# Linear attention on one core: the second matmul 128 wide, the output stored in 1 KB runs

## The chip, the cores and the metric

The kernel runs on one core of a Trainium2 chip. The metric is the device time of one execution in microseconds (us). All runs told here were in the fast state. Every profiled run is one execution; times are medians over several. Ratios of two kernels are computed as the mean time of one kernel's fast runs over the mean of the other's in the same rounds, with a 95% interval, so they are not quite the ratio of the medians quoted beside them. Two words are used throughout: a run is a stretch of contiguous bytes in DRAM, and a packet is one record of a DMA engine in the trace, which may carry several runs (the 5632 runs of the GpSimd stores of before went in 2816 packets).

## The reference

For each of 8 x 12 = 96 heads, with 512 rows of 64 elements in Q, K and V (fp32):

```python
Q_feat = np.maximum(0, Q) + 1
K_feat = np.maximum(0, K) + 1
KV = np.einsum('bhkd,bhkv->bhdv', K_feat, V)
K_sum = np.sum(K_feat, axis=2)
numerator = np.einsum('bhqd,bhdv->bhqv', Q_feat, KV)
denominator = np.einsum('bhqd,bhd->bhq', Q_feat, K_sum)
return (numerator / (denominator[:, :, :, None] + 1e-10)).astype(np.float32)
```

It reads 37.75 MB and writes 12.58 MB.

## The kernel before

Twelve groups of eight heads. Loads go from GpSimd's queue and cast fp32 to bf16 on the way: 16 rows of a head per partition, so runs of 4 KB in DRAM. Q is transposed on TensorE; ScalarE copies the transposes from PSUM to `qt`, and the second matmul takes slices of `qt` as its stationary operand. The order in which `qt` is filled decides how many consecutive rows of a head meet in one output partition: with two row halves interleaved it is eight rows, 2 KB of fp32.

```python
        qt = mid_pool.tile([P, C, P, 2], BF16, name="qt")          # C = 8
        for half in range(2):
            qt_ps = psum_qt.tile([P, C, P], BF16, name="qt_ps")
            for c in range(C):
                nc.tensor.transpose(qt_ps[:, c, :], qf[:, half * C + c, :, :], identity)
            nc.scalar.copy(out=qt[:, :, :, half], in_=qt_ps)        # every second element
# ... (output: 32 matmuls of 64 columns per group, then on VectorE
#      4 reciprocals and 4 multiplies into o_sb [P, 4, 8, 64] fp32) ...
    def store(g):
        o_sb = outs.pop(g)
        o_to = o_dram[:, g * NP : g * NP + NP]      # runs of C rows: 2 KB
        if g < NG - 1:
            nc.gpsimd.dma_start(out=o_to, in_=o_sb) # eleven of these
            return
        for h in range(2):                          # last group: two halves from SP
            nc.sync.dma_start(out=o_to[:, h:NP:2], in_=o_sb[:, h:NP:2])
```

A store of group g is issued three groups after its features were made, and up to eight GpSimd DMAs are in flight (19.4 to 19.9 us from issue to landing, at 2.485 us for each). So of the eleven GpSimd stores about four run between loads (60 to 103 us), and the others, with the two SP stores, follow one another after the last load. That last part I call the pure-store stretch.

Of the kernel before, what the change touches and what calls it, by code (L numbers as in the profile page):

```python
# [8 lines left out]
FP32 = mybir.dt.float32  # L9
BF16 = mybir.dt.bfloat16  # L10
ALU = mybir.AluOpType

BANK = 512
# [5 lines left out]
@with_exitstack  # L19
def kernel(  # L20
    ctx: ExitStack,
    tc: tile.TileContext,
    Q: bass.AP,
    K: bass.AP,
    V: bass.AP,
    out: bass.AP,
):






    nc = tc.nc

    B, H, S, D = Q.shape
    P = 128
    C = 8
    C2 = 2 * C
    NPAIR = B * H * S // (P * C)  # L40
    NP = 4
    NG = NPAIR // NP
    D1 = D + 1
    W = 2 * D1

    def view(t, c):
        return t.flatten_outer_dims().rearrange("(n p c) d -> p n c d", p=P, c=c)

    q_dram = view(Q, C2)
    k_dram = view(K, C2)  # L50
    v_dram = view(V, C2)
    o_dram = view(out, C)

    const = ctx.enter_context(tc.tile_pool(name="const", bufs=1))
    head_pool = ctx.enter_context(tc.tile_pool(name="head_pool", bufs=1))
    in_pool = ctx.enter_context(tc.tile_pool(name="in_pool", bufs=IN_BUFS))
    feat_pool = ctx.enter_context(tc.tile_pool(name="feat", bufs=2))
    mid_pool = ctx.enter_context(tc.tile_pool(name="mid", bufs=3))
    out_pool = ctx.enter_context(tc.tile_pool(name="out_pool", bufs=OUT_BUFS))
    recip_pool = ctx.enter_context(tc.tile_pool(name="recip", bufs=4))  # L60
    psum = ctx.enter_context(tc.tile_pool(name="psum", bufs=3, space=bass.MemoryType.PSUM))
    psum_qt = ctx.enter_context(tc.tile_pool(name="psum_qt", bufs=2, space=bass.MemoryType.PSUM))

    identity = const.tile([P, P], BF16, name="identity")
    NV = 2
    v_aug = [const.tile([P, C2, W], BF16, name=f"v_aug{i}") for i in range(NV)]
    kva_diag = [const.tile([P, 4, 2, D1], BF16, name=f"kva_diag{i}") for i in range(NV)]

    raw = {}
    feat = {}  # L70
    qts = {}
    outs = {}

    def load(g):
        first = g == 0
        k_raw = (head_pool if first else in_pool).tile(
            [P, 2, C2, D], FP32 if first else BF16, name="k_raw"
        )
        v_raw = in_pool.tile([P, 2, C2, D], BF16, name="v_raw")
        q_raw = in_pool.tile([P, 2, C2, D], BF16, name="q_raw")  # L80
        (nc.sync if first else nc.gpsimd).dma_start(  # L81
            out=k_raw, in_=k_dram[:, g * 2 : g * 2 + 2]
        )
        nc.gpsimd.dma_start(out=v_raw, in_=v_dram[:, g * 2 : g * 2 + 2])  # L84
        nc.gpsimd.dma_start(out=q_raw, in_=q_dram[:, g * 2 : g * 2 + 2])  # L85
        raw[g] = (k_raw, v_raw, q_raw)

    def store(g):
        o_sb = outs.pop(g)
        o_to = o_dram[:, g * NP : g * NP + NP]  # L90
        if g < NG - 1:
            nc.gpsimd.dma_start(out=o_to, in_=o_sb)  # L92
            return
        for h in range(2):
            nc.sync.dma_start(out=o_to[:, h:NP:2], in_=o_sb[:, h:NP:2])

    def feature(dst, src):
        nc.vector.tensor_scalar(  # L98
            out=dst, in0=src, scalar1=1.0, scalar2=1.0, op0=ALU.add, op1=ALU.max
        )  # L100

    def features(g):
        k_raw, v_raw, q_raw = raw.pop(g)
        kf = feat_pool.tile([P, C2, 2, D], BF16, name="kf")
        qf = feat_pool.tile([P, C2, 2, D], BF16, name="qf")
        va = v_aug[g % NV]
        for half in range(2):
            cs = slice(half * C, half * C + C)
            feature(kf[:, cs].rearrange("p c n d -> p n c d"), k_raw[:, :, cs])
            nc.scalar.copy(  # L110
                out=va[:, cs].rearrange("p c (n x) -> p n c x", n=2)[:, :, :, 0:D],
                in_=v_raw[:, :, cs],
            )
        for half in range(2):
            cs = slice(half * C, half * C + C)
            feature(qf[:, cs].rearrange("p c n d -> p n c d"), q_raw[:, :, cs])
        feat[g] = (kf, qf)

    def kv_and_transpose(g):
        kf, qf = feat.pop(g)  # L120
        va = v_aug[g % NV]
        kva_ps = [psum.tile([P, 2, BANK], FP32, tag="ps", name="kva_ps") for _ in range(2)]
        for c in range(C2):
            for b in range(4):
                ps = slice(32 * b, 32 * b + 32)
                nc.tensor.matmul(  # L126
                    kva_ps[b // 2][:, b % 2, 0:W],
                    lhsT=kf[ps, c, :, :],
                    rhs=va[ps, c, :],
                    start=(c == 0),  # L130
                    stop=(c == C2 - 1),
                )
        kva = kva_diag[g % NV]
        for n in range(2):
            ps = slice(64 * n, 64 * n + 64)
            for h in range(2):
                nc.scalar.copy(  # L137
                    out=kva[ps, 2 * h : 2 * h + 2, n, :],
                    in_=kva_ps[h][ps, :, D1 * n : D1 * n + D1],
                )  # L140

        qt = mid_pool.tile([P, C, P, 2], BF16, name="qt")
        for half in range(2):
            qt_ps = psum_qt.tile([P, C, P], BF16, name="qt_ps")
            for c in range(C):
                nc.tensor.transpose(qt_ps[:, c, :], qf[:, half * C + c, :, :], identity)  # L146
            nc.scalar.copy(out=qt[:, :, :, half], in_=qt_ps)  # L147
        qts[g] = qt

    def output(g):  # L150
        kva = kva_diag[g % NV]
        qt = qts.pop(g)
        o_sb = out_pool.tile([P, NP, C, D], FP32, name="o_sb")
        for h in range(2):
            ops = [psum.tile([P, 2, BANK], FP32, tag="ps", name="o_ps") for _ in range(2)]
            for c in range(C):
                for j in range(2):
                    b = 2 * h + j
                    nc.tensor.matmul(  # L159
                        ops[c // 4][64 * j : 64 * j + 64, c // 2 % 2, (c % 2) * W : (c % 2) * W + W],  # L160
                        lhsT=qt[:, c, 32 * b : 32 * b + 32, :],
                        rhs=kva[:, b],
                        start=True,
                        stop=True,
                    )
            for i in range(2):
                cells = ops[i][:, :, 0 : 2 * W].rearrange("p b (c n x) -> p b c n x", n=2, x=D1)
                recip = recip_pool.tile([P, 2, 2, 2, 1], FP32, name="recip")
                nc.vector.reciprocal(out=recip, in_=cells[:, :, :, :, D:D1])  # L169
                nc.vector.tensor_tensor(  # L170
                    out=o_sb[:, h:NP:2, 4 * i : 4 * i + 4].rearrange(
                        "p n (b c) d -> p b c n d", b=2
                    ),
                    in0=cells[:, :, :, :, 0:D],
                    in1=recip.to_broadcast([P, 2, 2, 2, D]),
                    op=ALU.mult,
                )
        outs[g] = o_sb

    with tc.manual_schedule():  # L180
        for g in range(IN_BUFS):
            load(g)
            if g == 0:
                make_identity(nc, identity)
                for t in kva_diag:
                    nc.gpsimd.memset(t, 0.0)  # L186
                for t in v_aug:
                    nc.gpsimd.memset(t[:, :, D::D1], 1.0)  # L188
        for g in range(NG - 1):
            features(g)  # L190
            if g >= 1:
                kv_and_transpose(g - 1)
            if g >= 2:
                output(g - 2)
            if g + IN_BUFS < NG:
                load(g + IN_BUFS)
            if g >= LAG:
                store(g - LAG)
        kv_and_transpose(NG - 2)
        output(NG - 3)  # L200
        features(NG - 1)
        output(NG - 2)
        kv_and_transpose(NG - 1)
        output(NG - 1)
        for g in range(NG - 1 - LAG, NG):
            store(g)
# [30 lines left out]
```

## Time and profile before

| | before |
|---|---|
| median time | 128.35 us (127.55 to 128.37, 3 runs) |
| span in the profile | 126.5 us |
| share of the span: PE, ACT, DVE | 53%, 51%, 45% |
| GpSimd's DMA queue, share of 16 engines | 99.9% |
| ScalarE copy to qt | 1298 ns |
| last multiply ends / last DMA packet ends | 118.84 / 125.21 us |

Read it from the last row upwards: the compute engines are idle about half of the time, the DMA engines hardly ever, and the end comes 6 us after the last computation. The lines themselves stand in the prediction.

One more view of before will be the yardstick, since most of what follows happens from 108 to 120 us. It is the busy time of the engines in that stretch. Its columns are the stretch, its length, PE, PEld, DVE, ACT and POOL busy (with instruction counts), then the TensorE clock, the DMA share and the GB/s moved:

```profile
108.00:120.00 12.00, 5.93 (x120) 4.67 (x118) 5.53 (x13) 3.31 (x6) 0.75 (x1) 0.64 1.03 415
```

The DMA share of 1.03 says that all 16 engines have packets open throughout; 415 GB/s is what they move with nothing but stores.

### The profile page before, as it was taken

The page shows a single profiled execution, that of the slowest core. Times are in us where ns is not written, and L with a number is a line of the kernel's source. Part 1 is how long each engine was busy: PE and PEld are TensorE (multiplying, and loading weights), DVE is VectorE, ACT ScalarE, POOL GpSimd, SP SyncE. Part 2 cuts the span into 40 slices and gives each one's busy share as a digit, 9 for nine tenths or more (in the row PEclk, how much of TensorE's full clock was granted, in tenths as well). Part 3 has the DMA queues.
Part 4 walks back from the last instruction along what each step waited for, and adds up shares of the span by engine and source line. Part 5 has one row for each costly group of instructions (what it writes and reads, how often), then busy time and mean ns, then how long its engine had stood idle before and what let it go on. Part 6 is the DMA issues. An engine that isn't in the chain of part 4 may idle for free.

```text
span 126.5 us, 3107 instructions
## 1 busy us (share of the span) xinstructions
PE 67.4 (53%) x1344; PEld 54.8 (43%) x1344; DVE 57.3 (45%) x144; ACT 64.1 (51%) x97; POOL 35.2 (28%) x56
## 2 busy tenths in 40 slices
PE   0009139147949486674648547737916972674000
PEld 0009028036838275562537435626714851563000
DVE  0122222058292865919377067147229079805500
ACT  4041095393966939397590492293096592073000
POOL 6992233222332242233223322332221202010000
PEclk9999999999995958679985555555555577569555
DMA  3999999999999999999999999999999999999990
GB/s 75 340 211 208 212 211 213 208 212 210 214 208 211 212 209 214 209 215 208 251 336 212 229 358 209 212 365 214 210 338 249 215 306 418 420 422 405 409 356 33
DMA packets 13341, 32.17 MB, mean 254 GB/s; under 512 B 784, under 2 KB 784, under 8 KB 13328
## 3 DMA queue, kind: packets, MB, share of 16 engines
q0 software_dynamic: 12512, 29.89, 99.9%
q1 hardware_dynamic: 816, 2.10, 4.6%
q8 instruction: 10, 0.16, 0.5%
q14 instruction: 3, 0.02, 0.0%
HBM read 37.75 MB, written 12.58 MB: 398 GB/s over the span
## 4 chain that ended last, share of the span: by engine, by line
DMA 61%; DVE 13%; PE 8%; POOL 5%; issue 3%; ACT 2%; ACTq 1%; POOLq 0%; DVEq 0%
DMA q_raw<-in_Q_dram 46%; DMA v_raw<-in_V_dram 15%; DVE o_sb L170 9%; PE kva_ps L126 5%; PE qt_ps L146 2%; DVE recip L169 2%; DVE qf L98 2%; POOL v_raw L84 1%; POOL q_raw L85 1%; ACT qt L147 1%; POOL k_raw L81 1%; ACTq L232 1%; ACT v_aug L110 1%; PE o_ps L159 1%; POOL kva_diag L186 1%
## 5 line engine op out<-in xcount | busy, mean ns | idle before, releaser
L110 ACT COPY v_aug<-v_raw 128x1024 bf16<-128x1024 bf16 x24 | 24.1, 1056 | 40.5 <-DMA v_raw<-in_V_dram 40.4
L159 PE MATMUL o_ps<-kva_diag,qt 128*64 128x130 bf16 x384 | 22.9, 269 | 26.7 <-ACT kva_diag L137 15.9
L126 PE MATMUL kva_ps<-v_aug,kf 32*128 32x130 bf16 x768 | 24.6, 294 | 22.8 <-ACT v_aug L110 13.0
L170 DVE TENSOR_TENSOR o_sb<-o_ps,recip 128x512 f32<-128x512 f32 x48 | 33.2, 691 | 1.7
L126 PEld LDWEIGHTS <-kf 32*128 32x128 bf16 x768 | 19.7, 132 | 26.9 <-issue 14.6
L159 PEld LDWEIGHTS <-qt 128*64 128x64 bf16 x384 | 16.6, 137 | 32.7 <-issue 19.1
L147 ACT COPY qt<-qt_ps 128x1024 bf16<-128x1024 bf16 x24 | 29.5, 1298 | 0.5
L98 DVE TENSOR_SCALAR qf<-q_raw 128x1024 bf16<-128x1024 bf16 x24 | 9.4, 434 | 39.0 <-DMA q_raw<-in_Q_dram 39.0
L146 PE MATMUL qt_ps<-identity,qf 128*128 128x128 bf16 x192 | 21.4, 301 | 0.0
L146 PEld LDWEIGHTS <-qf 128*128 128x128 bf16 x192 | 18.5, 140 | 2.3 <-issue 2.0
L92 POOL DMA_DIRECT2D out_dram<-o_sb x11 | 8.4, 767 | 27.9 <-DVE o_sb L170 13.6
L98 DVE TENSOR_SCALAR kf<-k_raw 128x1024 bf16<-128x1024 bf16 (+1 forms) x24 | 9.7, 446 | 12.2 <-DMA k_raw<-in_K_dram 12.2
L137 ACT CAST kva_diag<-kva_ps 64x130 bf16<-64x130 f32 x48 | 10.2, 262 | 9.1 <-PE kva_ps L126 8.8
L169 DVE RECIPROCAL recip<-o_ps 128x8 f32<-128x8 f32 x48 | 9.5, 197 | 8.7 <-PE o_ps L159 8.7
L84 POOL DMA_DIRECT2D v_raw<-in_V_dram x12 | 8.7, 726 | 16.8 <-ACT kva_diag L137 7.3
L85 POOL DMA_DIRECT2D q_raw<-in_Q_dram x12 | 8.6, 720 | 15.8 <-DMA q_raw<-in_Q_dram 5.3
L81 POOL DMA_DIRECT2D k_raw<-in_K_dram x11 | 7.9, 714 | 15.4 <-DMA v_raw<-in_V_dram 8.2
L110 ACT ACT_TABLE_LOAD x1 | 1.3, 1283 | 0.7 <-PEq L221 0.7
L186 POOL MEMSET kva_diag<- 128x520 bf16 x2 | 1.0, 528 | 0.0
L188 POOL MEMSET v_aug<- 128x32 bf16 x2 | 0.4, 278 | 0.0
masks.py:199 POOL TENSOR_SCALAR_AFFINE_SELECT identity<-identity 128x128 bf16<-128x128 bf16 x1 | 0.3, 288 | 0.1
masks.py:197 POOL MEMSET identity<- 128x128 bf16 x1 | 0.2, 232 | 0.0
(4 smaller groups left out, 0.4 us busy)
## 6 DMA issues: line engine op xcount, KB each, us to landing
out_dram<-o_sb POOLq DMA_DIRECT2D x11, 1024.0 KB, 19.9
v_raw<-in_V_dram POOLq DMA_DIRECT2D x12, 512.0 KB, 19.4
q_raw<-in_Q_dram POOLq DMA_DIRECT2D x12, 512.0 KB, 19.4
k_raw<-in_K_dram POOLq DMA_DIRECT2D x11, 512.0 KB, 19.4
k_raw<-in_K_dram SPq DMA_DIRECT2D x1, 1024.0 KB, 4.9
out_dram<-o_sb SPq DMA_DIRECT2D x2, 512.0 KB, 6.9
```

What stands on the lines that cost most here:

```text
L81: (nc.sync if first else nc.gpsimd).dma_start(out=k_raw, in_=k_dram[:, g * 2 : g * 2 + 2])
L84: nc.gpsimd.dma_start(out=v_raw, in_=v_dram[:, g * 2 : g * 2 + 2])
L85: nc.gpsimd.dma_start(out=q_raw, in_=q_dram[:, g * 2 : g * 2 + 2])
L98: nc.vector.tensor_scalar(out=dst, in0=src, scalar1=1.0, scalar2=1.0, op0=ALU.add, op1=ALU.max)
L110: nc.scalar.copy(out=va[:, cs].rearrange("p c (n x) -> p n c x", n=2)[:, :, :, 0:D], in_=v_raw[:, :, cs],)
L126: nc.tensor.matmul(kva_ps[b // 2][:, b % 2, 0:W], lhsT=kf[ps, c, :, :], rhs=va[ps, c, :], start=(c == 0), stop=(c == C2 - 1),)
L137: nc.scalar.copy(out=kva[ps, 2 * h : 2 * h + 2, n, :], in_=kva_ps[h][ps, :, D1 * n : D1 * n + D1],)
L146: nc.tensor.transpose(qt_ps[:, c, :], qf[:, half * C + c, :, :], identity)
L147: nc.scalar.copy(out=qt[:, :, :, half], in_=qt_ps)
L159: nc.tensor.matmul(ops[c // 4][64 * j : 64 * j + 64, c // 2 % 2, (c % 2) * W : (c % 2) * W + W], lhsT=qt[:, c, 32 * b : 32 * b + 32, :], r ...
L169: nc.vector.reciprocal(out=recip, in_=cells[:, :, :, :, D:D1])
L170: nc.vector.tensor_tensor(out=o_sb[:, h:NP:2, 4 * i : 4 * i + 4].rearrange("p n (b c) d -> p b c n d", b=2), in0=cells[:, :, :, :, 0:D], i ...
```

## The change

The intent: an output matmul of 128 columns in place of two of 64, with half as many matmuls (192 for 384). For that, four row quarters are interleaved in `qt` and not two halves, so an output partition holds four consecutive rows of a head, 1 KB, of eight heads. The store reads the same 8 KB of a partition and writes it in eight pieces, not four.

```diff
-    o_dram = view(out, C)
+    o_dram = view(out, R)                      # R = 4
...
-        for h in range(2):
-            nc.sync.dma_start(out=o_to[:, h:NP:2], in_=o_sb[:, h:NP:2])
+        for n in range(2):
+            hs = slice(4 * n, 4 * n + 4)
+            nc.sync.dma_start(out=o_to[:, hs], in_=o_sb[:, hs])
...
-        qt = mid_pool.tile([P, C, P, 2], BF16, name="qt")
+        qt = mid_pool.tile([P, R, P, 4], BF16, name="qt")
...
-            nc.scalar.copy(out=qt[:, :, :, half], in_=qt_ps)
+            nc.scalar.copy(
+                out=qt[:, :, :, 2 * half : 2 * half + 2].rearrange("p r m u -> p u r m"),
+                in_=qt_ps.rearrange("p (u r) m -> p u r m", u=2),
+            )
...
-        for h in range(2):
-            ops = [psum.tile([P, 2, BANK], FP32, tag="ps", name="o_ps") for _ in range(2)]
-            for c in range(C):
-                for j in range(2):
-                    b = 2 * h + j
-                    nc.tensor.matmul(... 64 columns: lhsT=qt[:, c, 32 * b : 32 * b + 32, :] ...)
+        for b in range(4):
+            o_ps = psum.tile([P, 2, BANK], FP32, tag="ps", name="o_ps")
+            for r in range(R):
+                nc.tensor.matmul(... 128 columns: lhsT=qt[:, r, 32 * b : 32 * b + 32, :] ...)
```

(The VectorE instructions keep their number and shapes.)

More of the change, by code (lines that the diff above doesn't have):

```diff
@@ L39 @@
     C2 = 2 * C
-    NPAIR = B * H * S // (P * C)
-    NP = 4
-    NG = NPAIR // NP
+    R = 4
+    NH = 8
+    NG = B * H // NH
     D1 = D + 1
@@ L89, in store @@
         o_sb = outs.pop(g)
-        o_to = o_dram[:, g * NP : g * NP + NP]
+        o_to = o_dram[:, g * NH : g * NH + NH]
         if g < NG - 1:
@@ L152, in output @@
         qt = qts.pop(g)
-        o_sb = out_pool.tile([P, NP, C, D], FP32, name="o_sb")
-        for h in range(2):
-            ops = [psum.tile([P, 2, BANK], FP32, tag="ps", name="o_ps") for _ in range(2)]
-            for c in range(C):
-                for j in range(2):
-                    b = 2 * h + j
-                    nc.tensor.matmul(
-                        ops[c // 4][64 * j : 64 * j + 64, c // 2 % 2, (c % 2) * W : (c % 2) * W + W],
-                        lhsT=qt[:, c, 32 * b : 32 * b + 32, :],
-                        rhs=kva[:, b],
-                        start=True,
-                        stop=True,
-                    )
-            for i in range(2):
-                cells = ops[i][:, :, 0 : 2 * W].rearrange("p b (c n x) -> p b c n x", n=2, x=D1)
-                recip = recip_pool.tile([P, 2, 2, 2, 1], FP32, name="recip")
-                nc.vector.reciprocal(out=recip, in_=cells[:, :, :, :, D:D1])
-                nc.vector.tensor_tensor(
-                    out=o_sb[:, h:NP:2, 4 * i : 4 * i + 4].rearrange(
-                        "p n (b c) d -> p b c n d", b=2
-                    ),
-                    in0=cells[:, :, :, :, 0:D],
-                    in1=recip.to_broadcast([P, 2, 2, 2, D]),
-                    op=ALU.mult,
-                )
+        o_sb = out_pool.tile([P, NH, R, D], FP32, name="o_sb")
+        for b in range(4):
+            o_ps = psum.tile([P, 2, BANK], FP32, tag="ps", name="o_ps")
+            for r in range(R):
+                nc.tensor.matmul(
+                    o_ps[:, r // 2, (r % 2) * W : (r % 2) * W + W],
+                    lhsT=qt[:, r, 32 * b : 32 * b + 32, :],
+                    rhs=kva[:, b],
+                    start=True,
+                    stop=True,
+                )
+            cells = o_ps[:, :, 0 : 2 * W].rearrange("p i (r n x) -> p i r n x", n=2, x=D1)
+            recip = recip_pool.tile([P, 2, 2, 2, 1], FP32, name="recip")
+            nc.vector.reciprocal(out=recip, in_=cells[:, :, :, :, D:D1])
+            nc.vector.tensor_tensor(
+                out=o_sb[:, b:NH:4].rearrange("p n (i r) d -> p i r n d", i=2),
+                in0=cells[:, :, :, :, 0:D],
+                in1=recip.to_broadcast([P, 2, 2, 2, D]),
+                op=ALU.mult,
+            )
         outs[g] = o_sb
```

## The prediction

> **What bounds the kernel now.** I read the page's slices first, then the DMA queues, the chain of waits, the busy time in chosen stretches, and last the single DMA packets (the trace holds start, duration and size of each).
>
> ```profile
> DMA  3999999999999999999999999999999999999990
> GB/s 75 340 211 208 212 211 213 208 212 210 214 208 211 212 209 214 209 215 208 251 336 212 229 358 209 212 365 214 210 338 249 215 306 418 420 422 405 409 356 33
> DMA packets 13341, 32.17 MB, mean 254 GB/s; under 512 B 784, under 2 KB 784, under 8 KB 13328
> q0 software_dynamic: 12512, 29.89, 99.9%
> q1 hardware_dynamic: 816, 2.10, 4.6%
> q8 instruction: 10, 0.16, 0.5%
> HBM read 37.75 MB, written 12.58 MB: 398 GB/s over the span
> ```
>
> The DMA row is at 9 from the second slice to the last but one. GB/s shows 210 in the load stages only because a load reads fp32 and lands bf16; on the fp32 side it moves 420, the same as the pure stores at the end. So there is one limit for both: 16 engines that always have work.
>
> ```profile
> DMA 61%; DVE 13%; PE 8%; POOL 5%; issue 3%; ACT 2%; ACTq 1%; POOLq 0%; DVEq 0%
> PE 67.4 (53%) x1344; PEld 54.8 (43%) x1344; DVE 57.3 (45%) x144; ACT 64.1 (51%) x97; POOL 35.2 (28%) x56
> ACT v_aug L110 <- DMA v_raw<-in_V_dram: 40.4, 11, 6.1
> DVE qf L98 <- DMA q_raw<-in_Q_dram: 39.0, 11, 5.2
> out_dram<-o_sb POOLq DMA_DIRECT2D x11, 1024.0 KB, 19.9
> q_raw<-in_Q_dram POOLq DMA_DIRECT2D x12, 512.0 KB, 19.4
> ```
>
> The chain, the engines' busy shares, the longest waits (total, times, longest) and the DMA issues say the same: no compute engine passes 53%, ScalarE and VectorE wait some 40 us each for inputs, and a DMA lands 19.4 to 19.9 us after issue because about eight are queued ahead (8 x 2.485 us, the step of one DMA in the packet records). The chain goes through compute only after the last load, around 94 to 119 us.
>
> The end, as busy time in stretches (PE, PEld, DVE, ACT, POOL, then clock, DMA share, GB/s):
>
> ```profile
> 105.00:113.00 8.00, 4.84 (x96) 4.06 (x96) 5.15 (x13) 1.47 (x6) 1.50 (x2) 0.58 1.02 419
> 119.00:122.00 3.00, 0.00 (x0) 0.00 (x0) 0.00 (x0) 0.00 (x0) 0.00 (x0) 0.50 1.02 399
> 122.00:123.00 1.00, 0.00 (x0) 0.00 (x0) 0.00 (x0) 0.00 (x0) 0.00 (x0) 0.50 0.90 348
> 123.00:124.00 1.00, 0.00 (x0) 0.00 (x0) 0.00 (x0) 0.00 (x0) 0.00 (x0) 0.50 0.32 123
> 124.00:125.50 1.50, 0.00 (x0) 0.00 (x0) 0.00 (x0) 0.00 (x0) 0.00 (x0) 0.50 0.09 36
> ```
>
> All compute is over at 118.84 us, but the stores queued before keep the DMA full to 122. Then only few engines still work: the last packet starts at 125.20. The end is set by the engine with the most work. The completion packets (4 B, one per engine and DMA) show why engines differ: up to 20 us all 16 finish a DMA within 0.25 us; after each 16 KB packet of the instruction queue (durations 892 to 1025 ns, from 21.8 to 113.7 us) one engine is about 1 us later, and stays so. At the last queued store two engines are 3 us behind the first (122.94 and 123.43 against 119.88); the third last is at 121.24. These two seem to have had two such fetches each (the ninth and tenth, at 101.0 and 113.7 us, fell on engines already late).
>
> [...] the GpSimd stores have DRAM runs of 2 KB but packets of 4096 B, 159 ns each, exactly as long as the single-run 4 KB packets of the first K load (159 ns); two runs in a packet cost no more than one. The SP stores go one run per packet: 2 KB in 84 ns. [...] the queue shows ten 16 KB packets. [...]
>
> **The change part by part.**
>
> Bytes: loads, store bytes, number of DMAs and their order on every queue are the same, so the 46 GpSimd DMAs still take 46 x 2.485 = 114.3 us of each engine if packets cost the same.
>
> GpSimd stores: each DMA has 1024 runs of 1 KB in place of 512 of 2 KB. SBUF rows are 8 KB contiguous in both. I expect 4096 B packets again, of four runs. Cost, if runs inside a packet stay free: 0. [...] The measured 159 against 159 speaks for the first, so I count +0.4. The issue on GpSimd goes from 720 ns (256 runs) and 767 (512) to an estimated 0.86 us, far under the 2.485 us between DMAs: hidden.
>
> SP stores, the last 1 MB: 84 ns for 2 KB and 159 for 4 KB make 75 ns per 2 KB and 9 per packet, so 1 KB takes about 46.5. Per engine 64 x 46.5 = 2.98 us against 32 x 84 = 2.69: +0.3, on the path. Besides, the split is now by head half, and each half needs all four VectorE multiplies; before, the first half went at 117.2 us after two of four, the second at 118.9. Now both wait for 118.84, and their packets start some 2 us after issue as now (117.2 to 119.5), near 121. The early engines, done with queued stores at 119.7, idle about a microsecond and finish near 121.1 + 3.0 = 124.1. That sets a floor of about 124.1 against today's 125.2, so the later issue is hidden only by the late engines.
>
> TensorE: 192 output matmuls of 128 columns replace 384 of 64, each with its weight load. The transposes, with 128-column weights too, run 16 in 1.89 us, 118 ns each; so 16 output matmuls take about 1.9 us where 32 took 1.2 to 2.0. No gain, and no cost, as TensorE waits anyway. VectorE: the same 48 reciprocals (197 ns) and 48 multiplies (691 ns), strides alike. ScalarE: the 24 copies to qt now write every fourth element in place of every second, 8 B steps[...]: 1298 ns again. If they slowed by 30%, the last two would put 0.8 us in front of the last output.
>
> Instruction stream: [...] So 8 or 9 fetches in place of 10. If only 8, no engine takes two, and the latest engine drops from 3 us behind to about 1.4: queued stores done near 121.3, then 3.0 of SP stores, end near 124.2, so -1.0. If the ninth still comes [...], one engine stays late: its 123.43 less some 0.9 us of SP packets mixed in, plus 2.98, gives 125.5: +0.3. I call it even: -0.35.
>
> Sum: +0.4 (runs) -0.35 (fetches and SP stores together) +0.1 (ScalarE or issue) = +0.15, on 128.35: 128.5 us.
>
> **The rivals.**
>
> First, 1 KB runs are slow: packets fall to two runs (2 KB, 84 ns), or each run costs. For: SP packets show 9 ns per packet. Against: 159 equals 159 with two runs. Packets of 2 KB would add 9 ns to each of 176 packets per engine, 1.6 us: 130. A store rate down by 10%, say from DRAM, would add 2.7 us on the 27.3 us of eleven stores: 131.
>
> Second, fewer fetches win: the last packet near 124.2 and stores at the old rate: 127.4. For: the lag of the late engines is plain in the trace. Against: the later SP issue leaves a floor right there.
>
> Third, compute at the end is later, through slower ScalarE copies or wider matmuls; then both SP stores slip as one: up to 129.2.
>
> Fourth, the DMA hides everything and nothing moves: 128.3.
>
> **Range and chances.** The extremes I take seriously are -1.0 with free runs and +1.6 with costly ones: 127.4 to 130.0 for 8 in 10. Two per cent is 2.57 us. Faster by that needs more than the whole late tail: 0.02. [...] Within: 0.90.
>
> **What would show it.** Runs: the size and duration of the store packets (4096 B and 159 ns expected), and GB/s in the pure store stretch, 419 before. SP stores: packets of 1 KB, near 46 ns, in count 1024, first issue after the last multiply. Fetches: the instruction queue's packets, 10 before, and the gap from the first to the last engine at the last queued store. ScalarE: the mean of the qt copy. TensorE: 118 ns per output matmul. I am wrong if the packets shrink, if the store stretch falls below 400 GB/s, or if the DMA share has a hole before 119 us.

## The result

The changed kernel took 129.91 us (129.79 to 129.95, 4 runs) against 128.03 us (127.55 to 128.37, 4 runs): ratio 1.0148, interval 1.0106 to 1.019. It is slower by about 1.5%, inside the 2% that counts as the same and inside the predicted range, though close to its upper end.

The page after the change, lines that answer to those shown of before. The slices, 3.2 us each:

```profile
DMA  2999999999999999999999999999999999999993
GB/s 93 330 210 211 210 212 212 208 210 213 210 211 211 210 213 209 212 212 212 318 265 210 283 301 212 258 326 212 240 344 212 224 394 401 362 337 332 346 337 109
DMA packets 13853, 32.16 MB, mean 251 GB/s; under 512 B 785, under 2 KB 1809, under 8 KB 13841
q0 software_dynamic: 12512, 29.89, 100.3%
q1 hardware_dynamic: 1328, 2.10, 4.5%
q8 instruction: 9, 0.15, 0.4%
```

The DMA row is as full as before. Up to slice 32 the rate is the same as before, or nearly: 210 in the loads, 240 to 340 where stores lie between loads. Then, in the pure-store stretch, before had 418 420 422 405 409 356 and this has 401 362 337 332 346 337. The number of packets on q0 has not changed by one (12512), so the GpSimd stores still go in packets of 4096 B, four runs in each; q1, SP's queue, has 512 more, as its two stores now go in 1024 packets of 1 KB in place of 512 of 2 KB.

The stretches at the end, for comparison with those in the prediction, and the yardstick stretch:

```profile
119.00:122.00 3.00, 0.16 (x2) 0.00 (x0) 1.93 (x5) 0.00 (x0) 0.00 (x0) 0.50 0.98 342
122.00:123.00 1.00, 0.00 (x0) 0.00 (x0) 0.00 (x0) 0.00 (x0) 0.00 (x0) 0.50 0.97 339
124.00:125.50 1.50, 0.00 (x0) 0.00 (x0) 0.00 (x0) 0.00 (x0) 0.00 (x0) 0.50 0.95 338
125.50:127.00 1.50, 0.00 (x0) 0.00 (x0) 0.00 (x0) 0.00 (x0) 0.00 (x0) 0.50 0.35 122
...
108.00:120.00 12.00, 5.99 (x98) 4.75 (x96) 4.30 (x11) 5.55 (x6) 0.89 (x1) 0.64 1.01 349
```

The DMA share is about 1 here as well, and yet only 340 to 350 GB/s move: the engines are not waiting for work, each packet takes longer (from 112 to 119 us the GpSimd stores' packets have a median of 194 ns against 160 in before). The last packet ends at 126.94 us in place of 125.21, which is the whole difference of the two profiled spans (128.2 and 126.5 us).

There was a second surprise, on ScalarE. Groups of instructions, with busy us and the mean ns of one; the first line is of the changed kernel:

```profile
L147 ACT COPY qt<-qt_ps 128x1024 bf16<-128x1024 bf16 x24 | 56.6, 2487 | 0.5
```

and the same group before:

```profile
L147 ACT COPY qt<-qt_ps 128x1024 bf16<-128x1024 bf16 x24 | 29.5, 1298 | 0.5
```

The shapes are equal; only the step between written elements grew from 4 to 8 B, and the copy takes 1.9 times as long. The last two copies are in the chain before the last output, so the SP stores, issued at 117.2 and 118.9 us before, are now issued at 121.0 us. Before, then after:

```profile
117.19 2.05 SPq L95 DMA_DIRECT2D out_dram<-o_sb  x2
```

```profile
121.03 1.69 SPq L95 DMA_DIRECT2D out_dram<-o_sb  x2
```

That makes two candidates, and they come together in this kernel. Theory R: the 1 KB runs slow the stores of the pure-store stretch. Theory S: the slow copies delay the last stores, and that is what the end shows.

### The profile page after: what moved, and what is told of

Read it like the earlier page. It is cut to its first block, busy times and chain, and to the rows that moved or that the text cites. A ratio compares the mean times of both kernels' runs of the same rounds, so it can differ in the third digit from the quotient of the medians.

```text
span 128.2 us, 2723 instructions
## 1 busy us (share of the span) xinstructions
PE 66.7 (52%) x1152; PEld 55.0 (43%) x1152; DVE 57.6 (45%) x144; ACT 90.7 (71%) x97; POOL 36.8 (29%) x56
## 3 DMA queue, kind: packets, MB, share of 16 engines
q0 software_dynamic: 12512, 29.89, 100.3%
## 4 chain that ended last, share of the span: by engine, by line
DMA 60%; DVE 13%; PE 8%; POOL 5%; ACT 3%; issue 3%; ACTq 2%; POOLq 0%; DVEq 0%
DMA q_raw<-in_Q_dram 45%; DMA v_raw<-in_V_dram 15%; DVE o_sb L170 9%; PE kva_ps L126 4%; PE qt_ps L146 2%; ACT qt L147 2%; DVE qf L98 2%; DVE recip L169 2%; ACTq L230 2%; POOL v_raw L83 1%; POOL q_raw L84 1%; POOL k_raw L80 1%; PE o_ps L160 1%; ACT v_aug L110 1%; POOL kva_diag L184 1%
## 5 line engine op out<-in xcount | busy, mean ns | idle before, releaser
L147 ACT COPY qt<-qt_ps 128x1024 bf16<-128x1024 bf16 x24 | 56.6, 2487 | 0.5
L160 PE MATMUL o_ps<-kva_diag,qt 128*128 128x130 bf16 x192 | 22.6, 273 | 27.7 <-ACT kva_diag L137 13.2
L126 PE MATMUL kva_ps<-v_aug,kf 32*128 32x130 bf16 x768 | 25.2, 300 | 22.6 <-ACT v_aug L110 12.9
L126 PEld LDWEIGHTS <-kf 32*128 32x128 bf16 x768 | 20.3, 135 | 27.1 <-issue 14.5
L160 PEld LDWEIGHTS <-qt 128*128 128x128 bf16 x192 | 16.7, 124 | 32.0 <-issue 14.7
L91 POOL DMA_DIRECT2D out_dram<-o_sb x11 | 10.0, 905 | 25.8 <-DVE o_sb L170 13.2
```

What stands on the lines that cost most here:

```text
L126: nc.tensor.matmul(kva_ps[b // 2][:, b % 2, 0:W], lhsT=kf[ps, c, :, :], rhs=va[ps, c, :], start=(c == 0), stop=(c == C2 - 1),)
L147: nc.scalar.copy(out=qt[:, :, :, 2 * half : 2 * half + 2].rearrange("p r m u -> p u r m"), in_=qt_ps.rearrange("p (u r) m -> p u r m", u=2),)
L160: nc.tensor.matmul(o_ps[:, r // 2, (r % 2) * W : (r % 2) * W + W], lhsT=qt[:, r, 32 * b : 32 * b + 32, :], rhs=kva[:, b], start=True, stop ...
```

## The experiments

All kernels that change the placement of output rows give a wrong result on purpose; they move the same bytes. For each I also computed the median duration of the 4096 B store packets between 112 and 119 us from the trace's packet records.

### Runs and copies apart

**e1: the kernel before, GpSimd stores in 1 KB runs, nothing else.**

```diff
-            nc.gpsimd.dma_start(out=o_to, in_=o_sb)
+            nc.gpsimd.dma_start(out=view(out, C // 2)[:, g * 2 * NP : (g + 1) * 2 * NP],
+                                in_=o_sb.rearrange("p n (a c) d -> p (n a) c d", a=2))
```

> The kernel before, with only the eleven GpSimd stores cut into 1 KB runs of DRAM (placed as the changed kernel places them, so the result is wrong on purpose; copies, matmuls and the two SP stores as before). Theory R (the 1 KB runs slow the pure-store stretch at the end, from 419 to about 340 GB/s): store packets of 4096 B with a median near 190 ns in the last 15 us, last packet about 1.5 us later than before, 129.3 to 129.8 us. Theory S (the slower ScalarE copies to qt, 2487 ns in place of 1298, delay the last multiply and with it the last stores; the packets get longer for another reason that goes with it): packets stay at 159 to 165 ns, 128.0 us as before.

Measured: 129.97 us, a little over the range that theory R gave, against 127.75, ratio 1.0163 (1.0127 to 1.0198); packets 193.5 ns, against 160 in before. The yardstick stretch of this kernel:

```profile
108.00:120.00 12.00, 5.67 (x120) 4.49 (x120) 5.59 (x13) 3.31 (x6) 0.89 (x1) 0.64 1.01 349
```

The same 349 GB/s as in the changed kernel, with ScalarE as before (3.31 us busy). The runs alone bring the whole loss.

**e2: the changed kernel, stores in 2 KB runs.** The slow copies stay.

```diff
-    o_dram = view(out, R)
+    o_dram = view(out, 2 * R)      # and "p (n a) c d -> p n (a c) d" on o_sb
```

> The changed kernel, with its stores in 2 KB runs of DRAM (the same SBUF bytes, wrongly placed on purpose); the slow ScalarE copies stay. Theory R: store packets back at 159 ns and 410 GB/s; the SP stores still issue at 121.0 us, their packets run about 122.2 to 125.2, end as before: 128.0 to 128.4 us. Theory S: as the changed kernel, 129.9 us.

Measured: 127.84 us against 127.75, ratio 1.0004 (0.9985 to 1.0023); packets 160 ns. Its yardstick stretch, then the end:

```profile
108.00:120.00 12.00, 6.28 (x98) 4.97 (x96) 4.30 (x11) 5.55 (x6) 0.75 (x1) 0.64 1.02 411
...
119.00:122.00 3.00, 0.14 (x2) 0.00 (x0) 1.91 (x5) 0.00 (x0) 0.00 (x0) 0.50 0.50 201
122.00:123.00 1.00, 0.00 (x0) 0.00 (x0) 0.00 (x0) 0.00 (x0) 0.00 (x0) 0.50 1.00 375
```

Here the delay of the copies can be seen: most engines finish the queued stores near 120 us and have a hole (DMA share 0.50) until the SP stores of 121.0 us arrive. Yet the kernel is not slower than before. The last packet ends at 124.83 us, for in before the latest DMA engines needed until 125.21 us anyway.

**e3: the changed kernel, dense copies.** `qt` is laid out so that a copy writes 32 adjacent elements at a time; the output rows are permuted.

```diff
-        qt = mid_pool.tile([P, R, P, 4], BF16, name="qt")
+        qt = mid_pool.tile([P, R, 4, 4, 32], BF16, name="qt")
-                out=qt[:, :, :, 2 * half : 2 * half + 2].rearrange("p r m u -> p u r m"),
+                out=qt[:, :, :, 2 * half : 2 * half + 2].rearrange("p r b u m -> p u (r b) m"),
```

> The changed kernel, with the copies to qt writing 32 adjacent elements (64 B) at a time in place of single elements 8 B apart (which permutes the output's rows inside each head: wrong on purpose); stores in 1 KB runs stay. The copy should take 1.3 us or less if the 8 B step is what doubled it. Theory R: the last multiply ends near 118.8 us, but the queued stores still end near 123 to 124, so the time stays at 129.3 to 129.9 us. Theory S: 128.0 us.

Measured: 129.94 us, ratio 1.0166 (1.0137 to 1.0196). The copy fell to 1015 ns and the SP stores were issued at 118.2 us, 2.9 us earlier, and nothing came of it; packets 194 ns. As the copy still goes over the output in the same two passes, it is the 8 B step that had made it slow:

```profile
118.17 1.79 SPq L95 DMA_DIRECT2D out_dram<-o_sb  x2
L147 ACT COPY qt<-qt_ps 128x1024 bf16<-128x1024 bf16 x24 | 23.1, 1015 | 0.5
```

**e6: both together, 2 KB runs and dense copies.**

> The changed kernel with both changes of before: stores in 2 KB runs and the dense copies (wrong on purpose). With 2 KB runs alone the queued stores were done before the late SP stores began (201 GB/s from 119 to 122 us). If the slow copies cost time only once the runs are no longer slow: SP stores issue at 118.2 us, the hole is gone, last packet near 124.0 in place of 124.8, so 127.0 to 127.4 us. If the latest DMA engine sets the end anyway: 127.8 us.

Measured: 127.75 us against 127.83, ratio 1.000 (0.998 to 1.002). The hole is gone, the time is that of before. So the hope of 127.0 to 127.4 us failed: filling the hole gains nothing.

```profile
119.00:122.00 3.00, 0.00 (x0) 0.00 (x0) 0.00 (x0) 0.00 (x0) 0.00 (x0) 0.50 1.02 399
```

Theory S has fallen. Slow copies cost nothing with 1 KB runs (e3) nor without (e2, e6). Theory R holds, from both sides.

### What in the 1 KB runs costs

**e4: 1 KB runs near one another.** As many runs of the same size, 2 KB apart in DRAM in place of 128 KB.

```diff
+    o_dram = out.flatten_outer_dims().rearrange(
+        "(q p f n e c) d -> p q f e n c d", p=P, f=2, n=NH, e=2, c=R)
```

> The changed kernel, with the eight 1 KB runs of a partition 2 KB apart in DRAM in place of 128 KB apart (wrong on purpose); as many runs, as small. If the number of runs costs: store packets and time as in the changed kernel, median near 190 ns at the end, 129.9 us. If the far addresses cost [...]: packets at 160 to 165 ns, about 410 GB/s at the end, 128.3 us.

Measured: 129.91 us, ratio 1.0162 (1.0126 to 1.0197), packets 194 ns. These addresses are as slow as the far ones; it is the number of runs, or their size.

**e5: 512 B runs, and e9: 4 KB runs,** both with the kernel before, edited as e1.

> The kernel before with its eleven GpSimd stores in runs of 512 B (wrongly placed on purpose), a second point for the cost of a run in the pure-store stretch. Theory F (a fixed supply of runs: about 47.5 ns for each run, however small, since 1 KB runs went at 190 ns per packet of four): eight runs per 4096 B packet take 380 ns, 170 GB/s, and the time is over 140 us. Theory P (a fixed price on each run, some 10 ns on top of its bytes, 190 = 4 x (37.6 + 10)): 8 x (18.8 + 10) = 230 ns, 285 GB/s, about 133 us.

> The kernel before with its GpSimd stores in 4 KB runs (wrongly placed on purpose), one run per packet: a further point of rate against size of run. If the price is per run and 2 KB still pays some of it: the last stretch goes from 411 to 416 or more GB/s and the time falls by 0.3 us (127.5). If 2 KB is already at the engines' limit: no change, 127.8 us.

Measured: e5 136.85 us against 127.83, ratio 1.0705 (1.0668 to 1.0743, 2 runs); e9 127.71 us against 128.37, ratio 0.9964 (0.9942 to 0.9985). Their yardstick stretches, e5 first:

```profile
108.00:120.00 12.00, 6.82 (x120) 5.47 (x120) 6.22 (x15) 3.31 (x6) 1.15 (x1) 0.52 0.99 271
```

```profile
108.00:120.00 12.00, 6.17 (x112) 5.07 (x112) 4.85 (x12) 3.31 (x6) 0.72 (x1) 0.50 1.02 417
```

| run in DRAM | runs per 4096 B packet | median packet, ns (112 to 119 us) | GB/s (108 to 120 us) | ratio to before |
|---|---|---|---|---|
| 4 KB (e9) | 1 | 159 | 417 | 0.9964 |
| 2 KB (before) | 2 | 160 | 415 | 1 |
| 1 KB (e1) | 4 | 193.5 | 349 | 1.0163 |
| 512 B (e5) | 8 | 238 | 271 | 1.0705 |

SP's packets of 2 KB and 4 KB (84 and 159 ns) put the bytes of a 4096 B packet at 2 x 75 = 150 ns, an estimate. What is left over in the medians is 44 ns for four runs and 88 for eight, so 11 ns a run, but 9 and 10 for one run and two. A fixed supply of runs (theory F), which would have made 380 ns, is out. A price on each run (theory P) comes near for the packet (230 ns expected), but its time was missed: 133 us expected, 136.85 measured. For e9 the first expectation was the better one: from 115 to 120 us the rate is 418 GB/s, against 411 in before.

The 11 ns are also not shown to be a price that each run pays, for the medians mix two things. In e1, from 112 to 119 us, the shortest tenth of the packets take 165 ns or less and the longest tenth 214 or more. The 165 ns stand there before the packets grow: from 105 to 108 us, at the start of the pure-store stretch, the median is 159 ns in before, 165 in e1 and 174 in e5. So two more runs in a packet cost 6 ns and six more 15, which is 2.5 to 3 ns each. The rest, up to 194 and 238 ns, is a slowing that comes on top, and what it is the packet records do not say.

### Why the packets grow only at the end

Between loads, from 60 to 100 us, the 1 KB store packets of the changed kernel have a median of 159 and a mean of 162.3 ns (160.1 in before). Only in the pure-store stretch do they grow much, and over several stores: the means of the eleven stores of e1, in order, are 162, 162, 161, 161, 161, 166, 178, 190, 197, 192, 187 ns.

**e7a and e7b: loads between the last stores.** Six useless loads are put between the last GpSimd stores, with 2 KB runs (e7a) and 1 KB runs (e7b).

```diff
+                if g + IN_BUFS >= NG:
+                    spare_load()            # k_raw <- K, read by nobody
                 store(g - LAG)
```

> The kernel before with six useless loads of K put between the last GpSimd stores, so that the end is no pure-store stretch any more: 6 x 2.485 = 14.9 us longer, 142.5 to 143.5 us. It is the base for the next run.

> The same with the GpSimd stores in 1 KB runs. If stores in 1 KB runs are slow only when they follow one another (a load in between, which writes half the bytes, lets the engines catch up): store packets stay near 165 ns, time within 0.5 us of the run before. If it is the end of the kernel, or stores in themselves, that makes them slow: packets near 190 ns and 1.5 to 2 us longer than the run before.

Measured: 144.10 us (over the expected 143.5) and 146.91 us, 2.8 us apart. But GpSimd had waited 11 to 12 us for the buffers of the spare loads and the queue ran short, so I repeated the pair with a buffer for each.

**e8a and e8b: the pair again, each spare load with a buffer of its own.**

> The pair of spare-load runs again, as GpSimd there waited up to 11 us for the buffers of the spare loads and the queue ran short; now each spare load has a buffer of its own. Base: the kernel before with six spare loads between the last stores, 128 + 14.9 = 142.9 us.

> The same with the GpSimd stores in 1 KB runs. If a load between two stores lets the engines catch up: within 0.6 us of the run before, loads and stores at 415 GB/s or more on the fp32 side from 105 to 130 us. If stores in 1 KB runs are slow whether or not a load lies between: 1.5 us or more above it.

Measured: 143.53 us and 146.62 us, 3.1 us apart (2.2% of the base). Part of their stretches, e8a and then e8b:

```profile
110.00:115.00 5.00, 3.31 (x68) 2.84 (x62) 0.14 (x1) 3.31 (x6) 1.37 (x2) 0.50 1.08 313
115.00:120.00 5.00, 1.93 (x32) 1.45 (x28) 3.31 (x8) 0.00 (x0) 1.48 (x2) 0.50 1.07 315
```

```profile
110.00:115.00 5.00, 3.31 (x58) 2.85 (x52) 0.08 (x1) 3.31 (x6) 1.61 (x2) 0.50 1.08 302
115.00:120.00 5.00, 1.38 (x22) 0.90 (x18) 3.23 (x8) 0.00 (x0) 1.61 (x2) 0.50 1.07 283
```

So my idea that a load lets the engines catch up is wrong for one load per store: the loss is as large as without. And it lies more in the loads than in the stores: per engine, the load packets of e8b take 1.35 us more in sum than those of e8a, the 4096 B store packets 0.58 us more. 28 load packets take 500 ns or more, against 2 in e8a (the median is 173), while the store packets from 112 to 119 us have a median of 159. A load packet holds one run, so a price on the runs of a packet does not explain this. It points to something that loads and stores share, which no run here isolates.

**e10: the first four stores in 4 KB runs, the other seven in 1 KB runs.** A rival was left: in e1 the slowing begins when each engine has been given about 1000 runs in all, which would point to a queue that slows once a certain total is reached.

```diff
+            if g < 4:
+                nc.gpsimd.dma_start(out=o_dram_4k[...], in_=...)   # 4 KB runs
+            else:
+                nc.gpsimd.dma_start(out=o_dram_1k[...], in_=...)   # 1 KB runs
```

> The kernel before with its first four GpSimd stores in 4 KB runs and the other seven in 1 KB runs (wrongly placed on purpose). With 1 KB runs throughout, the store packets began to lengthen at about 108 us, when each DMA engine had been given about 1000 runs (16 per load, 64 per store) in all. If it is the running total that slows the queue [...], this kernel reaches it 4 x 48 = 192 runs or three stores later, near 115 us: packets at 165 ns until then, and about 128.6 us. If it is the close succession of stores that brings the cost to light: onset at 108 us as before, median near 190 ns from 110 to 120 us, 129.5 to 130.0 us.

Measured: 129.37 us against 128.28, ratio 1.0089 (1.0062 to 1.0115). The means of the seven 1 KB stores are 161, 165, 170, 184, 195, 192, 185 ns; the same stores of e1 had 161, 166, 178, 190, 197, 192, 187. The growth begins with the same store as in e1 and lags by 1 to 2 us, less than the time of one store, not by three stores; so a fixed total is not what starts it. The second expectation is nearly met (the median from 110 to 120 us is 189 ns; the time is 0.13 us under its range). The ratio is below that of e1, each taken against before on its own chip, so the earlier 1 KB runs may count for something. What builds up, and where, stays open; no run here shows the inside of the queue.

No version beat the kernel before with a correct result. The only faster one, e9, needs 16 consecutive rows of a head in an output partition, which neither matmul's layout gives.

## Why the prediction was right or wrong

The time fell into the range, and the bound was named rightly: DMA packets, with all compute hidden. But the middle of the prediction was 1.4 us too low, and one term carries that. By the prediction's own sign, a store stretch below 400 GB/s, its account of the runs was wrong (349). That the range held, by 0.1 us, was partly luck: its upper end was made of +1.6 us for packets of two runs, which did not come, on a base of 128.35 us; against before in its own rounds (128.03) the change is +1.9 us, more than that.

- **GpSimd stores, the step that failed.** I wrote: "The measured 159 against 159 speaks for the first, so I count +0.4". The packets kept their 4096 B, as predicted, but not their 159 ns: in the last stretch they take 194, and this alone makes about +2.1 us (e1, 1.0163 of 127.75). One run against two in a packet did not foretell four. The +0.4 was an estimate; the packets show 6 ns for two more runs before they grow (165 against 159), and for the growth to 194 the sum had no term. Of the first rival's two forms, the shorter packets (130 us) did not come, and the lower store rate did: put at 10% on all eleven stores (131 us), it is 16% (349 against 415), but only on the later ones.
- **The extra issue time on GpSimd** was put at 0.86 us and measured 905 ns, hidden as said.
- **SP stores.** 1024 packets of 46 ns, as predicted (46.5). Both halves wait for the last multiply, as predicted. They were issued at 121.0 us and not near 118.9, for the slow copies came before that multiply (118.2 us in e3). The idle microsecond and its floor of 124.1 us did not come to matter, since the slower queued stores filled it (DMA share 0.98 from 119 to 122 us).
- **ScalarE.** "1298 ns again" was an estimate, as no trace had shown a copy with 8 B steps, and it was wrong: 2487. The rival that compute ends later came true, and cost nothing (e2, e3, e6).
- **TensorE.** Twelve output matmuls took 1.41 us at 101 us, 118 ns each, as predicted.
- **Instruction fetches.** The 8 or 9 were an estimate; ten fetches for the 2688 TensorE instructions of before would make 8.6 for the 2304 of the changed kernel. Nine 16 KB packets came (892 to 975 ns each), the ninth at 115.0 us. That is the branch to which I gave +0.3 and half the weight; the better one, with eight, did not come. e2 and e6, also with nine, are at 1.000, so no gain from one fetch fewer is seen in the time.

## What to carry to other kernels

When a kernel is bound by its DMA engines, look at the size of the contiguous DRAM run of each transfer before the size of the packet or of the SBUF row: in stores that followed one another, the same 4096 B packet had a median of 160 ns with two runs and 194 with four. Measure it in the stage where such transfers follow closely, as the packets grew little where three loads lay between two stores (162 ns on average). And a copy that doubles in time can be free (1298 to 2487 ns, ratio 1.0004 in e2) while a transfer of unchanged bytes is not (1.0163 in e1); undo each alone before blaming the one that looks worse on the page.
